# A decoder layer on one core: the input projection ends with a gate, attention's first keys, queries and scores are issued ahead of the samples' constants, and partial sums are added as they come

## The chip, the cores and the metric

The kernel runs on one core of a Trainium2 chip. The metric is device time in microseconds (us), the median of several runs of the same program. A core has TensorE (PE: matrix products into PSUM banks), VectorE (DVE), ScalarE (ACT), GpSimd (POOL) and SyncE (SP). Each engine works through its own list of instructions in order; semaphores between the lists make one wait for another. SP, ACT and POOL also issue DMAs, which move data between the core's memory and the chip's main memory.

## The reference

One layer of a decoder computes 1024 prompt tokens and 64 sample tokens (8 requests of 8 tokens, each with 4096 tokens in a paged cache). Cut to what matters here:

```python
h = rms_norm(x, norm1) * (1 + scale1) + shift1
z = h @ w_in
(q, kc, vc, ks, vs, kw, vw, gates, conv_bg, conv_cg, conv_h, pool_in) = jnp.split(z, IN_SPLITS, axis=-1)
q = rms_norm(q.reshape(B, T, N_KV_HEADS, Q_PER_KV, HEAD_DIM), q_gain)
...
k_cmp = rms_norm(compress(full[:, :, 0], cmp_pe[0], cmp_w1[0], cmp_w2[0]), k_gain[0])
v_cmp = compress(full[:, :, 1], cmp_pe[1], cmp_w1[1], cmp_w2[1])
o_cmp, p_cmp = cmp_attention(q, k_cmp, v_cmp, q_pos)
top_i, sel_ok = select_blocks(p_cmp, q_pos, -(-full.shape[1] // SLC_BLOCK))
o_slc = slc_attention(q, top_i, sel_ok, q_pos, full[:, :, 2], full[:, :, 3])
...
o_attn = (g[..., 0:1] * o_cmp + g[..., 1:2] * o_slc + g[..., 2:3] * o_win).reshape(B, T, ATTN_W)
u_ext = jnp.concatenate([conv_past, conv_cg * conv_h], axis=1)
y_conv = conv_bg * short_conv(u_ext, conv_w, conv_bias)
...
x = x + gate1 * (jnp.concatenate([o_attn, y_conv, y_pool], axis=-1) @ w_out)
h = rms_norm(x, norm2) * (1 + scale2) + shift2
x = x + gate2 * swiglu(h, w_up, w_down)
```

Attention has three branches: over keys that are compressed from blocks of 32 tokens, over blocks selected by the compressed scores, and over a sliding window of 512 tokens.

## The kernel before, in words

The layer runs in stages: norms and the input projection (with part of the compression of the samples' caches), attention of the prompt and of the samples side by side (with the rest of the compression), and the output projection with the feed-forward part. Products in fp32 are made as three products of split operands (`mm3`): an operand is split into a high part, written by ACT (`kh`, `qh`, `w_hi`, `mh`, L175), and a low part, written by DVE (`kl`, `ql`, `w_lo`, `ml`, L171).

The order of the work comes from a small planner in the kernel (`run`, `spawn`, `hold`, `use`, L59 on): each piece of work is a generator with a priority; the planner keeps an estimated clock for every engine and always continues the ready piece of lowest priority number. The framework's scheduler then fixes the list of each engine. What it decides is read from the lists, not from the order of the text.

**Input projection** (L884 to L956). The columns of `w_in` are handled in 16 tiles of 128, in the order of the list at L899; every tile is computed for three chunks of tokens (384, 384, 320). The consumer depends on the tile: `q0` to `q3`, `ks` and `kw` go through `head_norm`, which squares on ACT (L758), has PE average over a head (`h_sq,mean_h`), takes a root on ACT (L763), a RECIPROCAL on DVE (L766) and multiplies on DVE (L767). `cg`, `ch` and `bg` are the short convolution's three inputs: `cg` is copied by ACT, `ch` is multiplied and convolved on DVE, and `bg` is one DVE multiplication per chunk and a store. Two of these triples exist (0 and 1), and before the change they follow each other. While `q0` to `q3` run, a piece of work (`up_weights_ahead`, L959) forms split weights for the feed-forward part in the tiles `p_raw` and `p_hl` and stores them to main memory; `hold(formed == 2)` waits for it in the planner.

**Compression.** For each of the samples' 8 caches pages are loaded into `stream` buffers (L531, alternately by SP and POOL) and multiplied in "octets", which the trace shows as 32 rows of `bank<-stream`. The last compression of the prompt (`compress_prompt`, L592) has its matmuls in the projection stage.

**Attention** (`attention`, L1397). `masks` makes the masks of the prompt on POOL and DVE; `key_stacks` (L987) splits both key stacks, 1024 new and 64 compressed keys each; `query_parts` splits the first 128 queries; `constants3` and `sample_setup` (L1165) make the samples' constants; then the prompt's units start. A unit of `scores` (L1018) is one of 128 queries, half of the heads and a branch: PE multiplies keys and queries into two banks; DVE evicts with the mask added and a running minimum (L1068); ACT takes exp with a sum (L1080); DVE makes the gate over the sum (L1086); POOL scales `P` by it (L1090); PE transposes `P` (`ident,P`), and multiplies with the values.

**Samples** (L1296 to L1395). The samples are worked in four groups of two requests (`p`), with nine units each: eight of selected blocks and one of the window. A unit multiplies a loaded buffer (`unit`, or `stream` where one is free) with the queries `qb`, evicts, takes exp, transposes `e`, and multiplies with the values into one column of `part`. `sample_combine` starts after a group's last unit: it forms weights `cw`, then `co` as a sum of 12 columns (one TENSOR_SCALAR and 11 SCALAR_TENSOR_TENSORs, L1382), transposes it on PE, copies it to `smo` (L1389), and stores that to `mix_d` on SP's queue (L1393).

**Output projection** (L1446 on). Weights `w_raw` are loaded through three buffers on SP (L1443) and split; `mixc`, the mixers' outputs for 272 tokens, is fetched from `mix_d` (L1468: on SP for the first chunk, on ACT for the others) and split into `mh`, `ml`; ACT also issues the loads of the residual input, `x1a` and `x1b` (L1494).

## Time and profile before

| what | value |
|---|---|
| median of 3 runs | 1683.15 us (1681.12 to 1685.02) |
| profiled execution | 1672.63 us |
| its span, first to last instruction | 1671.0 us |
| mean granted TensorE clock | 0.977 of full speed |
| busy: PE, DVE, ACT, POOL | 93%, 65%, 47%, 40% of the span |
| DMA | 302.12 MB, mean 181 GB/s |

The durations below come from the one profiled execution; it ran 10.5 us below the median of the runs. Its span is what the time coordinates of the rows refer to. A row of a timeline has the start, the duration, the engine, the line of the kernel, the operation, the tiles (out<-in) and the shape; a bracket gives the engine's idle time ahead of the row and what ended it. "x32" stands for 32 alike instructions in succession. L12 is line 12 of the kernel before.

### The profile page before, as it was taken

The numbers are of one execution on the slowest core, as the hardware profiler recorded it, in microseconds if no ns is written. First come the engines' busy times: TensorE is split into PE (matmuls) and PEld (weight loads), VectorE is DVE, ScalarE is ACT, GpSimd is POOL, SyncE is SP. The second block draws the span as 40 slices with busy tenths as digits, with TensorE's granted clock in tenths as the row PEclk, the third lists the DMA queues.
The fourth block names the chain that finished last, engine by engine and source line by source line (L and its number), as shares of the span: only waits on it lengthen the run. The fifth ranks groups of instructions, "written<-read, shape, count | busy, mean of one in ns | idle before, by whom it ended". The sixth has DMA issues, their size and how long they took to land. (4 is left out here: it accounts for less than half of the span.)

```text
span 1671.0 us, 35661 instructions
## 1 busy us (share of the span) xinstructions
PE 1562.1 (93%) x12697; PEld 1391.8 (83%) x12697; DVE 1090.4 (65%) x2625; ACT 779.0 (47%) x1829; POOL 665.4 (40%) x789
## 2 busy tenths in 40 slices
PE   6899999997999899899599989999999999899998
PEld 2898997896777566566499989999999999899988
DVE  4723234777555666767579878777777775577695
ACT  3522115335765666666466534433434443344462
POOL 3120110114333123223013356554555455788695
PEclk9999999998999999999899999999999999999999
DMA  9585654425467363245685564446444335966553
GB/s 336 182 287 162 207 168 148 144 95 162 133 186 217 100 193 104 70 131 147 210 303 187 198 221 168 143 145 232 145 145 143 142 136 204 393 234 241 182 168 121
DMA packets 186834, 302.12 MB, mean 181 GB/s; under 512 B 26353, under 2 KB 114994, under 8 KB 186338
## 3 DMA queue, kind: packets, MB, share of 16 engines
q1 hardware_dynamic: 166786, 272.20, 49.1%
q0 software_dynamic: 5856, 16.24, 3.0%
q10 hardware_dynamic: 14016, 11.41, 2.2%
q8 instruction: 101, 1.65, 0.4%
q14 instruction: 75, 0.61, 0.1%
HBM read 233.43 MB, written 70.53 MB: 182 GB/s over the span
## 5 line engine op out<-in xcount | busy, mean ns | idle before, releaser
L139 PE MATMUL bank<-b_hi,w_hi 128*128 128x272 f32 x1232 | 351.8, 291 | 7.3 <-DVE f_g L1631 2.9
L139 PE MATMUL bank<-b_lo,w_hi 128*128 128x272 f32 x1232 | 353.8, 289 | 1.7 <-DVE b_lo L171 1.7
L139 PE MATMUL bank<-b_hi,w_lo 128*128 128x272 f32 x1232 | 348.9, 288 | 0.7 <-DVE w_lo L171 0.7
L139 PEld LDWEIGHTS bank<-b_hi,w_hi 128*128 128x128 f32 x1232 | 231.0, 189 | 10.6 <-ACT b_hi L175 4.7
L139 PEld LDWEIGHTS bank<-b_lo,w_hi 128*128 128x128 f32 x1232 | 232.8, 189 | 2.4 <-DVE b_lo L171 2.3
L139 PEld LDWEIGHTS bank<-b_hi,w_lo 128*128 128x128 f32 x1232 | 231.0, 189 | 0.9 <-DVE w_lo L171 0.9
L1090 POOL TENSOR_SCALAR P<-P,st 128x128 f32<-128x128 f32 (+10 forms) x192 | 109.5, 584 | 230.2 <-DVE st L1086 139.1
L171 POOL TENSOR_TENSOR w_s<-w_raw 128x512 f32<-128x512 f32 (+1 forms) x88 | 126.7, 1440 | 64.6 <-DVE w_lo L171 50.5
L171 DVE TENSOR_TENSOR w_lo<-w_raw,w_hi 128x512 fp32r<-128x512 f32 (+2 forms) x121 | 116.9, 975 | 53.8 <-ACT w_hi L175 50.7
L139 PEld LDWEIGHTS bank<-stream 128*128 128x128 f32 x1056 | 127.4, 198 | 17.9 <-issue 13.0
L175 ACT ACTIVATE w_hi<-w_raw 128x512 fp32r<-128x512 f32 (+2 forms) x122 | 80.9, 678 | 130.1 <-PE bank L139 78.2
L171 POOL TENSOR_TENSOR x<-x,d_m 128x272 f32<-128x272 f32 x144 | 126.6, 901 | 34.9 <-DVE x L1833 20.5
L139 PE MATMUL bank<-stream 128*128 128x128 f32 x1056 | 133.8, 284 | 6.2 <-DMA stream<-in_cacheA 5.7
L1080 ACT ACTIVATE P<-P,st 128x640 f32<-128x640 f32 (+12 forms) x192 | 112.7, 588 | 46.1 <-DVE st L1074 26.6
L139 PE MATMUL bank<-h_hi,w_hi 128*128 128x384 f32 (+1 forms) x384 | 130.1, 339 | 0.9 <-ACT py L879 0.6
L139 PE MATMUL bank<-g,w_hi 128*128 128x272 f32 x616 | 121.5, 293 | 8.3 <-DVE x L1833 6.5
L139 PE MATMUL bank<-h_hi,w_lo 128*128 128x384 f32 (+1 forms) x384 | 126.5, 330 | 0.0
L171 DVE TENSOR_TENSOR w_lo<-w_s,w_hi 128x512 fp32r<-128x512 f32 (+1 forms) x124 | 116.8, 944 | 14.8 <-ACT w_hi L175 12.6
L139 PE MATMUL bank<-h_lo,w_hi 128*128 128x384 f32 (+1 forms) x384 | 125.8, 328 | 0.0
L139 PE MATMUL bank<-g,d_hi 128*128 128x272 f32 x616 | 120.2, 291 | 2.6 <-DVE x L1833 1.7
L1833 DVE SCALAR_TENSOR_TENSOR x<-bank,mod,x 128x272 f32<-128x272 f32 (+1 forms) x192 | 87.3, 476 | 40.8 <-PE bank L139 35.5
L139 PEld LDWEIGHTS bank<-g,w_hi 128*128 128x128 f32 x616 | 98.2, 191 | 10.1 <-DVE x L1833 7.4
(371 smaller groups left out, 3732.3 us busy)
## 6 DMA issues: line engine op xcount, KB each, us to landing
g_d<-f_s SPq DMA_DIRECT2D x57, 544.0 KB, 3.3
g<-g_d SPq DMA_DIRECT2D x56, 544.0 KB, 6.3
wada<-in_wada SPq DMA_DIRECT2D x96, 256.0 KB, 5.4
stream<-in_cacheA SPq DMA_DIRECT2D x192, 128.0 KB, 3.2
w_raw<-in_wup SPq DMA_DIRECT2D x40, 512.0 KB, 4.5
unit<-in_cacheB SPq DMA_DIRECT2D x152, 128.0 KB, 2.4
stream<-in_cacheB SPq DMA_DIRECT2D x104, 128.0 KB, 2.4
w_raw<-in_wout SPq DMA_DIRECT2D x24, 512.0 KB, 4.6
```

What stands on the lines that cost most here:

```text
L139: return self.nc.tensor.matmul(out, lhsT, rhs, start=start, stop=stop, skip_group_check=chain)
L171: (self.nc.vector if eng == "dve" else self.nc.gpsimd).tensor_tensor(out, a, b, op=op)
L175: self.nc.scalar.activation(hi, src, AF.Copy)
L1080: nc.scalar.activation(Ps, Ps, AF.Exp, scale=-1.0, bias=sy[:, g, 0:1], accum_out=sy[:, g, 1:2])
L1090: nc.gpsimd.tensor_scalar(Ps, Ps, sy[:, g, 3:4], 0.0, op0=OP.mult, op1=OP.add)
L1833: nc.vector.scalar_tensor_tensor(out[:, :n], acc[:, :n], self.mod[:, 5, m, 0:1], out[:, :n], op0=OP.mult, op1=OP.add)
```

## The change

Five things move. (1) `compress_prompt` loads pages of the samples' compression right after its matmuls. (2) The projection's order becomes `kc vc cg0 ch0 bg0 p0 ks p1 kw q0 q1 cg1 ch1 q2 q3 bg1`, so that the last tile is a gate `bg1` instead of `q3`; the second convolution triple has a pool of its own, `conv1`, opened after the weights formed ahead. (3) `attention` loads ACT's exp table with a dummy instruction, `key_stacks` splits the first 128 new and the 64 compressed keys of the first stack, then the first queries, then the first 128 keys of the second stack, then the rest; the samples' constants and setup are issued after the planner has issued the first unit of scores. (4) `sample_combine` is started at the exp of a group's window unit: it adds ten columns when nine partial results are there, and the last column when its product is. (5) `smo` is stored on POOL's queue.

```diff
--- before.py
+++ after.py
@@ -613,6 +613,7 @@
                 self.mm(uv[:, kv, 0:P], self.w1[:, kv * KT + k, :], rv[:, kv, k], k == 0, k == KT - 1)
+        self.compress_load(EARLY * 4 + 1)
         r = self.compress_evac(uv[:, :, 0:P], vt, pre, 0, 8)
@@ -896,7 +897,7 @@
         self.zout = (zq_, zp_)
-        order = ["kc", "vc", "cg0", "ch0", "bg0", "cg1", "ch1", "bg1", "p0", "ks", "p1", "kw", "q0", "q1", "q2", "q3"]
+        order = ["kc", "vc", "cg0", "ch0", "bg0", "p0", "ks", "p1", "kw", "q0", "q1", "cg1", "ch1", "q2", "q3", "bg1"]
         self.ada2 = self.pool("ada2", "left")
@@ -937,11 +938,13 @@
             self.spawn(lambda: 0.9 if self.octets <= PACE * (self.z_steps - z0) else 1.5, self.compress_more())
+            def conv(cv, j):
+                st = dict(zip(("cg", "ch", "bg"), self.conv_steps(cv, j)))
+                return lambda nm, ch, acc, c0, n: st[nm[:2]](ch, acc)
             with self.pool("conv") as cv:
-                for j in range(2):
-                    st = dict(zip(("cg", "ch", "bg"), self.conv_steps(cv, j)))
-                    yield from tiles([n + str(j) for n in ("cg", "ch", "bg")],
-                                     lambda nm, ch, acc, c0, n: st[nm[:2]](ch, acc))
+                yield from tiles(["cg0", "ch0", "bg0"], conv(cv, 0))
             with self.pool("pooling") as pl:
@@ -951,8 +954,13 @@
                 self.spawn(0.6, self.up_weights_ahead(pp, 1))
-                yield from tiles(["q0", "q1", "q2", "q3"], qk)
+                yield from tiles(["q0", "q1"], qk)
                 yield from self.hold(lambda: self.formed == 2)
+            with self.pool("conv1") as cv:
+                step = conv(cv, 1)
+                yield from tiles(["cg1", "ch1"], step)
+                yield from tiles(["q2", "q3"], qk)
+                yield from tiles(["bg1"], step)
             yield from self.hold(lambda: self.prompt_at and self.heads == 18 and 5 in self.ada_at)
@@ -984,15 +992,23 @@
-    def key_stacks(self):
-        nc = self.nc
+    def key_parts(self, j, a, n):
+        kh, kl = self.K[j]
+        src = self.kcp[:, a:a + n] if a < 64 else self.ksw[:, j, a - 64:a - 64 + n]
+        self.split(kh[:, a:a + n], kl[:, a:a + n], src, n)
+    def key_stacks(self, ap):
+        self.key_parts(0, 64, P)
+        self.key_parts(0, 0, 64)
+        self.query_parts(ap, 0)
+        self.key_parts(1, 64, P)
         for j in range(2):
-            kh, kl = self.K[j]
-            for a, n, src in ((64, SEQ, self.ksw[:, j, 0:SEQ]), (0, 64, self.kcp)):
-                self.split(kh[:, a:a + n], kl[:, a:a + n], src, n)
-                yield max(self.t["dve"], self.t["act"]) - 1.0
-        self.stacks_at = max(self.t["dve"], self.t["act"])
+            self.key_parts(j, 64 + P, SEQ - P)
+        self.key_parts(1, 0, 64)
+        self.stacks_at = self.t["pe"] + 3.0
+        self.use("dve", 0.0, self.t["act"])
@@ -1090,6 +1106,7 @@
             yield 0.0
+        self.scored = u + 1
         self.spawn(0, self.values(pool, u, j, half, br, Pt, seg, ready + 0.1))
@@ -1171,8 +1188,6 @@
                 self.q[s, :, SEQ:].rearrange("p r (b t) -> p b r t", t=NT))
-        self.kn = pool.tile([P, 2, 64], F32, name="kn")
-        nc.vector.tensor_copy(self.kn, self.ksw[:, :, SEQ:])
         self.use("dve", 1.5)
@@ -1272,6 +1287,7 @@
         self.give("S", self.use("dve", 0.35, self.t["pe"]))
+        st["parts"] = st.get("parts", 0) + 1
@@ -1332,6 +1348,8 @@
             t = self.use("act", 0.36, t + 0.1, table="exp")
+            if x == 8:
+                self.spawn(2, self.sample_combine(pool, st, p))
             self.spawn(2, self.sample_values(pool, u, st, kv, e, nx, t + 0.2, src))
@@ -1349,16 +1367,20 @@
                         t == 0, t == 3)
-        self.give("a", self.evac(st["part"][:, nx], o[:, 0:P], P))
+        st["last_at"] = self.evac(st["part"][:, nx], o[:, 0:P], P)
+        self.give("a", st["last_at"])
         self.unit_free.append(src)
         self.u_done += 1
-        if u % 9 == 8:
-            yield from self.hold(lambda: self.u_done >= u + 1)
-            yield from self.sample_combine(pool, st, u // 9)
+        if nx < 9:
+            st["parts"] = st.get("parts", 0) + 1
+        else:
+            st["last"] = True
         nc = self.nc
+        yield from self.hold(lambda: st["parts"] == 9)
         nm, den, part, gr = st["nm"], st["den"], st["part"], st["gr"]
@@ -1378,9 +1400,12 @@
         nc.vector.tensor_scalar(o, part[:, 11], gr[:, 0:1], None, op0=OP.mult)
-        for c in range(11):
+        for c in (0, 1, 2, 3, 4, 5, 6, 7, 8, 10):
             nc.vector.scalar_tensor_tensor(o, part[:, c], w[:, c:c + 1], o, op0=OP.mult, op1=OP.add)
-        yield self.use("dve", 4.0, self.t["pe"]) + 0.5
+        yield self.use("dve", 3.7, self.t["pe"])
+        yield from self.hold(lambda: "last" in st)
+        nc.vector.scalar_tensor_tensor(o, part[:, 9], w[:, 9:10], o, op0=OP.mult, op1=OP.add)
+        yield self.use("dve", 0.3, st["last_at"]) + 0.2
         tr = yield from self.bank_of("S")
@@ -1390,26 +1415,30 @@
         self.give("S", self.use("dve", 0.4, self.t["pe"]))
-        nc.sync.dma_start(self.mix_d[:, 0:4, SEQ + 16 * p:SEQ + 16 * p + 16],
-                            mo.rearrange("p r b t -> p r (b t)"))
+        nc.gpsimd.dma_start(self.mix_d[:, 0:4, SEQ + 16 * p:SEQ + 16 * p + 16], mo.rearrange("p r b t -> p r (b t)"))
         self.combined = p + 1
     def attention(self, ap, kp_, opened):
+        with self.tc.issue_after(self.last_sqrt.ins):
+            self.nc.scalar.activation(self.warm, self.eps, AF.Exp)
+        self.table = "exp"
         self.masks(ap)
-        self.use("dve", 1.0)
-        yield from self.key_stacks()
-        self.query_parts(ap, 0)
-        with self.tc.issue_after(self.last_scale.ins):
-            self.constants3(ap)
-            self.sample_setup(ap)
-        self.use("dve", 5.0)
+        self.key_stacks(ap)
+        self.kn = ap.tile([P, 2, 64], F32, name="kn")
+        self.nc.vector.tensor_copy(self.kn, self.ksw[:, :, SEQ:])
         kp_.__exit__(None, None, None)
         self.spawn(lambda: 1.8 + self.v_done / 32, self.prompt_attention(pp))
+        yield from self.hold(lambda: self.scored >= 1)
+        self.constants3(ap)
+        self.sample_setup(ap)
+        self.use("dve", 4.0)
+        self.set_up = True
         self.spawn(share, self.compress(cp, batches, 0))
+        yield from self.hold(lambda: self.set_up)
         sp = opened.enter_context(self.pool("samp", "left"))
@@ -2122,7 +2151,10 @@
         self.cmp_tags = ("S", "a")
+        self.scored = 0
+        self.set_up = False
         with self.pool("att", "left") as ap:
+            self.warm = ap.tile([P, 1], F32, name="warm")
             self.K = [[ap.tile([P, 64 + SEQ], F32R, name=f"k{x}{j}") for x in "hl"] for j in range(2)]
```

The lists of the engines, as built, at the places that matter. PE behind the last matmul of the input projection's last tile (`h_hi`, `h_lo` are the normed input, `kh_…`, `kl_…` the key stacks: `kh_3506` before and `kh_3538` after are the first stack, `kh_3508` and `kh_3540` the second). Before, starting with the octet behind the norm's matmuls; the next row is an entry of 32 `stream` matmuls, that is two octets:

```order
L139 MATMUL bank<-stream 128x128 x16
L139 MATMUL bank<-kh_3506,qh 128x192 x2
L139 MATMUL bank<-kl_3507,qh 128x192 x2
L139 MATMUL bank<-kh_3506,ql 128x192 x2
L139 MATMUL bank<-kh_3506,qh 128x192 x2
L139 MATMUL bank<-kl_3507,qh 128x192 x2
L139 MATMUL bank<-kh_3506,ql 128x192 x2
L139 MATMUL bank<-kh_3508,qh 128x128 x2
L139 MATMUL bank<-kl_3509,qh 128x128 x2
L139 MATMUL bank<-kh_3508,ql 128x128 x2
L139 MATMUL bank<-kh_3508,qh 128x128 x2
L139 MATMUL bank<-kl_3509,qh 128x128 x2
```

The same place after the change:

```order
L139 MATMUL bank<-h_hi_102,w_lo 128x320
L139 MATMUL bank<-stream 128x128 x32
L139 MATMUL bank<-kh_3538,qh 128x192 x2
L139 MATMUL bank<-kl_3539,qh 128x192 x2
L139 MATMUL bank<-kh_3538,ql 128x192 x2
L139 MATMUL bank<-kh_3538,qh 128x192 x2
L139 MATMUL bank<-kl_3539,qh 128x192 x2
L139 MATMUL bank<-kh_3538,ql 128x192 x2
L139 MATMUL bank<-kh_3540,qh 128x128 x2
L139 MATMUL bank<-kl_3541,qh 128x128 x2
L139 MATMUL bank<-kh_3540,ql 128x128 x2
L139 MATMUL bank<-stream 128x128 x16
```

The two octets that followed the second stack's scores now stand ahead of the first stack's, in the place of one octet; a further octet stands between the two halves of the second stack's scores.

DVE ahead of the first scores' eviction (`kl_…` low parts of the key stacks, `ql` of the queries, `t_…` to `m_new` the samples' constants, `ISA P,st` the eviction). Before, the end of the constants and the first eviction:

```order
L342 SCALAR_TENSOR_TENSOR hind<-hi,hg 128x8
L1171 COPY qb<-q 64x8x32 x2
L314 SCALAR_TENSOR_TENSOR ok<-a,tv,ge 128x256
L323 TENSOR_SCALAR m_win<-w,tv 128x8
L304 COPY rsum<-eq 32x32 x4
L316 TENSOR_SCALAR m_new<-ok 128x256
L1068 ISA P,st<-bank,m_slc 128x128
L1068 ISA st 128x1
```

After the change, the same stretch; two copies of the compression (`pre`) stand between:

```order
L304 COPY rsum<-eq 32x32 x4
L314 SCALAR_TENSOR_TENSOR ok<-a,tv,ge 128x256
L331 TENSOR_SCALAR sel<-si 128x512
L340 TENSOR_SCALAR hg<-hi 128x8
L316 TENSOR_SCALAR m_new<-ok 128x256
L342 SCALAR_TENSOR_TENSOR hind<-hi,hg 128x8
L587 COPY pre<-bank 64x128
L588 COPY pre<-bank 64x128
L1084 ISA P,st<-bank,m_slc 128x128
L1084 ISA st 128x1
```

The constants still stand ahead of the first eviction.

ACT at the end of attention (`part` the evicted products of the last sample units, `w_hi` the output projection's weights, `x1a` the residual input, `mh` the mixers' outputs). Before:

```order
L161 ACTIVATE part<-bank 128x128
L175 ACTIVATE w_hi<-w_raw 128x512 x2
L161 ACTIVATE part<-bank 128x128
L175 ACTIVATE w_hi<-w_raw 128x512 x7
L1494 DMA x1a_10556<-in_xT 128x2x272 x3
L175 ACTIVATE mh<-mixc 128x272 x2
L1494 DMA x1a_10556<-in_xT 128x2x272
L175 ACTIVATE mh<-mixc 128x272 x2
L1494 DMA x1a_10557<-in_xT 128x2x272
L1468 DMA mixc<-mix_d 128x2x272
L1494 DMA x1a_10557<-in_xT 128x2x272
L1468 DMA mixc<-mix_d 128x2x272
```

After:

```order
L161 ACTIVATE part<-bank 128x128
L161 ACTIVATE spt<-bank 128x512
L161 ACTIVATE part<-bank 128x128 x2
L175 ACTIVATE w_hi<-w_raw 128x512 x8
L1523 DMA x1a_10566<-in_xT 128x2x272 x4
L1523 DMA x1a_10567<-in_xT 128x2x272 x2
L175 ACTIVATE mh<-mixc 128x272 x2
L175 ACTIVATE w_hi<-w_raw 128x512
L1523 DMA x1a_10567<-in_xT 128x2x272 x2
L175 ACTIVATE mh<-mixc 128x272 x2
```

Six loads of `x1a` instead of three now stand ahead of the first `mh`, and eight splits of weights ahead of those.

SP at the same place. Before:

```order
L531 DMA unit<-in_cacheB 128x256
L1293 DMA unit<-in_swinKV 128x2x1024
L1443 DMA w_raw<-in_wout 128x1024 x7
L1393 DMA mix_d<-smo 128x4x16
L1468 DMA mixc<-mix_d 128x2x272 x4
L1443 DMA w_raw<-in_wout 128x1024
```

After:

```order
L531 DMA stream<-in_cacheB 128x256
L1309 DMA stream<-in_swinKV 128x2x1024
L1472 DMA w_raw<-in_wout 128x1024 x6
L1497 DMA mixc<-mix_d 128x2x272 x4
L1472 DMA w_raw<-in_wout 128x1024 x2
L1542 DMA x_d<-x1a_10566 128x272
```

The store of `smo` is gone from SP's list, one `w_raw` load stands behind the fetches of `mixc`, and the last sample loads go into a `stream` buffer.

## Rows read from the trace of the kernel before

**Rows 1.** The page's busy table: each engine's busy time, share, instructions.

```profile
PE 1562.1 (93%) x12697; PEld 1391.8 (83%) x12697; DVE 1090.4 (65%) x2625; ACT 779.0 (47%) x1829; POOL 665.4 (40%) x789
```

**Rows 2.** Windows, all engines; columns in the first line, clock behind POOL.

```profile
core 0: us, PE busy (x) PEld busy (x) DVE busy (x) ACT busy (x) POOL busy (x), PEclk, DMA share, GB/s
373.50:391.50 18.00, 8.60 (x63) 7.22 (x61) 16.34 (x58) 6.13 (x11) 8.73 (x24) 0.72 0.51 147
391.50:396.00 4.50, 4.50 (x25) 4.49 (x25) 2.56 (x18) 4.02 (x24) 2.67 (x9) 0.59 0.41 119
400.00:800.00 400.00, 371.17 (x3753) 260.07 (x3752) 256.89 (x1105) 260.74 (x707) 126.18 (x217) 0.97 0.48 144
816.40:831.60 15.20, 0.47 (x1) 0.18 (x1) 7.78 (x18) 5.01 (x12) 0.00 (x0) 0.68 0.78 256
```

**Rows 3.** Timeline of PE at the transition: start, duration, instruction, [idle before <- releaser].

```profile
373.60 0.31 PE L139 MATMUL bank<-h_hi,w_lo 128*128 128x320 f32 x1
...
375.08 3.73 PE L139 MATMUL bank<-stream 128*128 128x128 f32 x32
...
379.79 0.35 PE L139 MATMUL bank<-kh,ql 64*128 64x192 f32 x2 [0.58 <-DVE ql L171]
385.30 0.53 PE L139 MATMUL bank<-kh,qh 64*128 64x192 f32 x2 [5.16 <-DVE q L767]
...
390.07 0.44 PE L139 MATMUL bank<-kh,qh 64*128 64x128 f32 x1 [3.66 <-DVE st L1068]
```

**Rows 4.** Timeline of DVE at the transition.

```profile
375.36 1.23 DVE L171 TENSOR_TENSOR kl<-kv__93,kh 128x1024 fp32r<-128x1024 f32 x1 [1.30 <-ACT kh L175]
...
380.26 4.55 DVE L766 RECIPROCAL h_sq<-h_sq 128x384 f32<-128x384 f32 x2
384.74 0.97 DVE L767 SCALAR_TENSOR_TENSOR q<-bank,qgain_s,h_sq 128x384 f32<-128x384 f32 x2
...
389.54 0.28 DVE L1068 CUSTOM_DVE_ANT_0 P<-bank,m_slc 128x128 f32<-128x128 f32 x1
```

**Rows 5.** Timeline of PE at the end of attention.

```profile
814.43 1.97 PE L139 MATMUL bank<-unit,spt 128*64 128x128 f32 x32 [0.65 <-DVE cs L1376]
823.27 0.47 PE L143 MATMUL bank<-ident,co 128*128 128x128 f32 x1 [6.88 <-DVE co L1382]
831.64 1.50 PE L139 MATMUL bank<-mh,w_hi 128*128 128x272 f32 x5 [7.89 <-ACT mh L175]
```

**Rows 6.** Timeline of ACT, one row of the transition and two of the end.

```profile
389.90 1.28 ACT L1080 ACT_TABLE_LOAD   x1 [11.41 <-issue]
...
824.41 1.55 ACTq L1494 DMA_DIRECT2D x1a<-in_xT  x3
831.16 0.43 ACT L175 ACTIVATE mh<-mixc 128x272 fp32r<-128x272 f32 x1 [6.19 <-DMA mixc<-mix_d]
```

**Rows 7.** Timeline of SP's queue at the end of attention.

```profile
808.16 16.01 SPq L1443 DMA_DIRECT2D w_raw<-in_wout  x7
826.09 0.38 SPq L1393 DMA_DIRECT2D mix_d<-smo  x1
826.52 2.05 SPq L1468 DMA_DIRECT2D mixc<-mix_d  x4
```

**Rows 8.** Lines of tile p_hl: duration min/median/max in ns, first and last start.

```profile
L980 SPq DMA_DIRECT2D w_d<-p_hl x1: 320/320/320, 352.3 to 352.3; - x1
```

**Rows 9.** Timeline of PE, the first matmul of the q tiles.

```profile
319.94 0.42 PE L139 MATMUL bank<-h_hi,w_hi 128*128 128x384 f32 x1 [0.35 <-DVE mod L394]
```

**Rows 10.** DMA issues, 805 to 835 us: KB each, median us to landing.

```profile
w_raw<-in_wout SPq DMA_DIRECT2D x7, 512.0 KB, 4.2
x1a<-in_xT ACTq DMA_DIRECT2D x8, 272.0 KB, 4.7
```

**Rows 11.** Timeline of POOL at the transition.

```profile
382.69 1.17 POOL L531 DMA_DIRECT2D stream<-in_cacheA  x2 [1.05 <-issue]
```

**Rows 12.** Waits of PE from 400 to 800 us: total, times, longest.

```profile
PE bank L143 <- POOL P L1090: 11.4, 5, 3.1
```

## The prediction

> **What bounds the kernel now.** I read the page's busy table first. TensorE (PE) is busy 93% of the span [rows 1], so time can come only from the stretches in which PE waits or runs at the lower of its two clock levels. The windows say where such stretches lie near the change [rows 2]: between the last projection matmul and the first steady attention work (373.5 to 391.5 us) PE works 8.60 of 18.00 us, and between attention's last matmul and the output projection's first (816.4 to 831.6) 0.47 of 15.20. In the 400 us between, PE lacks 400 − 371.17 = 28.8 us, in many small waits. The timelines of PE and of the engines that it waits for then give each wait its cause.
>
> Transition [rows 3]: the last projection matmul ends at 373.60 + 0.31 = 373.91 (call it E). PE then does the norm's matmuls, one compression octet (32 trace rows of `stream`, 3.73 us) and the first score matmuls, with idle pieces of 0.58, 5.16 and 3.66 us: 9.40 us in all. The waits are DVE's [rows 4]: it turns the last q tile's norm (two RECIPROCALs, 380.26 to 384.81, then q itself to 385.7), then builds constants, and evicts the first score only at 389.54, which is E + 15.6. The clock shows 0.72 over the stretch and 0.59 over the 4.50 us behind it [rows 2]. The clock's levels are 2.4 and 1.2 GHz: the 4.50 us lose 4.50 × (1 − 0.59) = 1.85, and of the busy time from 385.30 to 391.5 (6.2 us less the 3.66 of idle, 2.5, with overlaps up to 3) half is lost, 1.4. So **9.40 idle + 3.3 of clock = 12.7 us** is what the transition can return.
>
> End [rows 5]: the last weighted sum ends at 814.43 + 1.97 = 816.40 (call it X); PE waits 6.88 us for `co`, transposes it, and waits 7.89 us for `mh`; it starts the output projection at 831.64 = X + 15.24. `mh` itself waits for the `mixc` fetch [rows 6], which SP issues at 826.52 behind the store of `smo` [rows 7].
>
> **The change, part by part.**
>
> *Projection order.* The same matmuls run; gate bg1 instead of q3 comes last. What DVE does after E shrinks by RECIPROCAL and q of the last chunks, 380.26 to 385.7, 5.4 us [rows 4], and grows by two gate multiplications (128 × 384, nearest row: the 0.97 us of two q multiplications), 1.0. This is the largest piece of the transition. The second conv pool reuses the memory of `p_hl`, so that its first eviction waits for `p_hl`'s last store. That is issued at 352.3 [rows 8], 32.4 us after the first q matmul at 319.94 [rows 9]; with a landing of 4.2 to 4.7 us, as the loads have [rows 10], it is through near 37. The four q tiles took 54.0 us up to E, 13.5 each, so cg1's first chunk is done at 2.33 × 13.5 = 31.5 and waits some 5 us, while PE has two more chunks of cg1 (9 us) to cover it. I take 0; bounds −2 and +3.
>
> *First keys, queries and scores.* DVE's first key split waits no more for the 1024-wide `kh` (1.30 us [rows 4]) but for a 128-wide one: about 0.7 off. The splits come in more pieces, and two copies of the compression stand ahead of the first score: 0.8 on. But the order shows that the constants still stand on DVE **ahead** of the first score's eviction, though the text of the program issues them after it. So the first eviction goes from E + 15.6 to 15.6 − 5.4 + 1.0 − 0.7 + 0.8 = E + 11.3. PE has more to do till then: two octets of 3.73 us, twelve score matmuls in 1.3 (378.81 to 380.14) and the first half of K1's, 0.8: 9.6 us, behind a first wait of about 0.55 for DVE's gate. That leaves 11.3 − 9.6 − 0.55 = 1.1 till the eviction. The next octet needs two pages that POOL issues behind its masks; before, these went out at 382.69, E + 8.8, taking 1.17 [rows 11], and landings take 4.2 to 4.7 [rows 10], so E + 13 or so, another 1.2. For the first transposes of P, which one octet fewer covers, I add 0.9. Sum of idle: 0.55 + 1.1 + 1.2 + 0.9 = 3.7. Nothing in it is as long as the 5.16 us in which the clock fell; if the clock stays up, all 3.3 come back. Gain: 9.4 − 3.7 + 3.3 = 9.0; if the clock falls all the same, 5.7. I take **8**, nearer the upper end, since each piece of idle is shorter than the 3.66 us that followed that fall; bounds 5 and 11.
>
> *The exp table* (1.28 us) is loaded in ACT's idle time ahead of the splits: 0. The cover is the 11.41 us for which ACT stood idle before that load [rows 6].
>
> *Partial sums as they come.* Ten of the 11 products for `co` run ahead of the last weighted sum, so `co` should be ready 2 us behind X rather than 6.88. That would matter if `mh` waited for it. It waits for `mixc` columns of the prompt, and for SP and ACT. SP: the store moves to POOL. From SP's rows [rows 7] the store's own issue is 0.38 and SP stood from 824.17 (808.16 + 16.01) to 826.09 for its data: 1.9 + 0.4 = 2.3 us that `mixc` no longer waits.
> The Trainium skill ("DMA: Bandwidth & Descriptors", section "Issuing engines are not separate DMA queues") says that DMAs started by the sync, scalar and gpsimd engines run on the same 16 DMA engines, and that starting them from several engines saves only the sequencer's time to start them, which is usually small. By that rule the move would be worth the 0.4 us of the issue alone, and rival A below 1.9 us less (1671 rather than 1669); the rows say that the sequencer stood still as well, so I keep 2.3.
>
> The 2.3 us don't land in full, for the order shows two new waits. First, the last sample units now lie in `stream` buffers which the `w_raw` loads reuse: before, `w_raw` went out from 808.16, 8 us ahead of X; now the first waits for the last but one weighted sum (X − 1.0, half of the 1.97) and all others for the last. With landings of 4.2 us, splits of two halves, and three buffers, the third tile's split ends near X + 7.6, the sixth load goes out then, and `mixc` at X + 8.05 (before X + 10.1), landing near X + 13 (before X + 14.8). Second, ACT now issues six `x1a` loads ahead of the first `mh` (before, three); the fifth shares a semaphore lane with the first and waits for its landing. ACT gets to them when the fourth tile's weights are split, about X + 10.4; at 0.52 each (1.55 for three [rows 6]) and 4.7 us to landing [rows 10] the fifth goes at X + 15.6, and `mh` follows with 0.43: PE restarts near **X + 16.2**, a loss of 1.0. Bounds: −2 (ACT not held, `mixc` at X + 13) and +4 (landings of 7).
>
> *The middle.* All sample work between is dealt anew by the planner, with the same matmuls. I take 0 of its 28.8 us of idle; from waits of at most 3.1 us there [rows 12], bounds −6 and +6.
>
> **Sum:** −8 + 1 + 0 + 0 = −7 us on the profiled 1672.63, so 1665.6. That execution lies 10.5 us below the median of the three runs, 1683.15; the same difference gives **1676**. About 0.2% (3.4 us) is what a measurement of this kernel can tell from no change.
>
> **The rivals.**
>
> A. *The end opens too.* If the `w_raw` loads land as early as before and ACT is not held by `x1a`, only the `mixc` fetch behind X counts. For it speaks that the longest wait of the kernel (7.89) hangs on nothing but queue order; against it, the order of ACT and the buffers' reuse. PE would restart near X + 9, 6 to 7 us earlier; with the transition −14: 1669. Chance 0.17.
>
> B. *The stall only moves.* DVE's constants still precede the first eviction, and the scores wait behind them; PE then idles in one long piece before the third octet, if its pages land at E + 17 instead of 13, and the clock falls again. The transition returns 3 to 4 us, the end takes 1 to 2, net −2: 1681. For it: POOL has all masks to make before it issues the pages, as before. Chance 0.20.
>
> C. *Slower: the new deal in the middle starves the transposes of P.* They wait for POOL's scaling of P, 11.4 us in five waits, 2.3 each [rows 12]. The sample side starts later now and its units fall elsewhere between the prompt's; where a unit's transposes come with no sample work ahead, such a wait is open. It decides from (7 + 3.4) / 2.3, some 4.5 more waits on, which is twice as many as before; with five, +11.5 − 7 = +4.5: 1687.6. Against it: PE's queue has the same filler in sum. Chance 0.13.
>
> **How the numbers follow.** The forecast has 0.50, its own range 1671 to 1681 (−12 to −2); 0.05 of it lies within 0.2%. Faster: 0.45 + 0.17 = 0.62, and 0.01 from B's better end, 0.63; same: 0.05 + 0.19 = 0.24; slower: 0.13. The range reaches into A (down to 1667, two thirds of it) and C (up to 1686).
>
> **What would show it.** In the profile after: between the last projection matmul and the second group of P's transposes, idle pieces that sum to about 4 us and a granted clock near 1; two octets in a row straight behind the gate; the first score evicted near E + 11. At the end `co` within 2 us of the last weighted sum, and yet a first output-projection matmul near X + 16, waiting for ACT's `mh`, whose own wait is the ACT queue. I am wrong if that restart comes before X + 12, if the transition shows a half-clock stretch, or if PE's idle between 400 and 800 differs by over 6 us.

## The result, and the profile after

The changed kernel takes 1690.3 us (median of 20 runs, 1683.18 to 1696.07), the kernel before 1680.87 (20 runs): the ratio is 1.006, interval 1.0047 to 1.0073. The change costs some 10 us where 7 were to be gained. The profiled execution of the changed kernel took 1688.57 us (span 1687.0).

The first profile of the kernel before, on which the prediction rests, was a quick execution: 1672.63 us against its median of 1680.87. Both kernels were therefore profiled a second time (e13, e17). E is the end of the last projection matmul, T the first transposes of P, X the last weighted sum of the samples, R the first matmul of the output projection.

| stretch | before | before, 2nd | after | after, 2nd | difference of the means |
|---|---|---|---|---|---|
| start to 75 us | 75.0 | 75.0 | 75.0 | 75.0 | 0 |
| 75 us to E | 298.9 | 299.5 | 311.7 | 312.9 | +13.1 |
| E to T | 26.7 | 26.8 | 23.4 | 22.5 | −3.8 |
| T to X | 415.8 | 424.1 | 421.6 | 426.8 | +4.3 |
| X to R | 15.2 | 15.9 | 17.7 | 17.2 | +1.9 |
| R to the end | 839.4 | 843.3 | 837.7 | 838.6 | −3.2 |

The stretches sum to +12.3 us, the medians say +9.4. The largest loss lies ahead of E, in the projection; the transition gives back less than a third of it (it now also holds a further octet, 3.7 us, which stood behind T before). The two executions of one kernel differ by up to 8.3 us in the stretch T to X, most of it at half clock, so small differences there prove nothing.

The transition after, as PE's timeline shows it ([rows 3] are the same place before):

```profile
387.24 7.41 PE L139 MATMUL bank<-stream 128*128 128x128 f32 x64 [0.58 <-DVE cy L811]
394.58 0.36 PE L139 MATMUL bank<-kh,qh 64*128 64x192 f32 x2
...
396.74 0.29 PE L139 MATMUL bank<-kh,qh 64*128 64x128 f32 x1 [1.17 <-DVE st L1084]
...
399.63 6.20 PE L139 MATMUL bank<-stream 128*128 128x128 f32 x32 [2.37 <-DMA stream<-in_cacheA]
```

DVE's first score eviction behind the gate's last multiplication ([rows 4]), and POOL's page loads ([rows 11]):

```profile
386.69 0.49 DVE L811 TENSOR_TENSOR cy<-cy,bank 128x320 f32<-128x320 f32 x1 [2.96 <-PE bank L139]
...
396.21 0.29 DVE L1084 CUSTOM_DVE_ANT_0 P<-bank,m_slc 128x128 f32<-128x128 f32 x1
```

```profile
395.11 1.16 POOL L531 DMA_DIRECT2D stream<-in_cacheA  x2 [1.05 <-DMA stream<-in_cacheA]
396.96 1.12 POOL L531 DMA_DIRECT2D stream<-in_cacheA  x2 [0.70 <-issue]
```

E is 386.66 here. Three idle pieces, 0.58 + 1.17 + 2.37 = 4.12 us, stand where 9.40 stood; the third octet waits for its pages and starts at E + 12.97. It then takes 6.20 us instead of 3.7: the clock fell after all (granted clock 0.59 from 399.6 to 405.8 us).

The projection, in windows of both kernels (the first number is the window's length, the second PE's busy time; the first of the last three is the granted clock). Before:

```profile
78.00:92.00 14.00, 14.00 (x104) 14.00 (x104) 3.79 (x10) 4.16 (x7) 5.46 (x6) 1.00 0.93 312
125.00:135.00 10.00, 6.05 (x40) 5.55 (x40) 1.52 (x6) 2.77 (x5) 0.23 (x1) 0.83 0.79 243
208.00:226.00 18.00, 18.00 (x133) 16.56 (x133) 9.11 (x19) 3.48 (x5) 3.64 (x6) 1.00 0.42 111
270.00:326.00 56.00, 52.50 (x315) 42.28 (x314) 34.74 (x52) 23.26 (x44) 6.35 (x11) 1.00 0.50 160
```

After:

```profile
78.00:92.00 14.00, 14.00 (x95) 14.00 (x94) 3.50 (x10) 4.16 (x7) 5.26 (x6) 0.88 0.92 304
125.00:135.00 10.00, 5.14 (x26) 4.98 (x25) 1.91 (x6) 3.09 (x6) 1.08 (x2) 0.66 0.90 264
208.00:226.00 18.00, 15.56 (x85) 10.17 (x78) 8.09 (x11) 4.90 (x7) 0.55 (x1) 0.81 0.43 127
270.00:326.00 56.00, 49.96 (x329) 41.37 (x320) 34.45 (x46) 32.63 (x54) 9.18 (x10) 1.00 0.61 209
```

With busy × (1 − clock) as the loss at half clock, the four windows lose 1.7, 4.86 + 1.75, 2.44 + 2.96 and 6.04 us against 0, 3.95 + 1.03, 0 and 3.50: 11.3 us more. With q3's norm matmuls, 1.5 us that now lie ahead of E, that is 12.8, near E's shift of 386.66 − 373.91 = 12.75; that it comes so close is luck, for the windows were picked. (The first window's 1.7 is chance: the second profile of before has it too.) What stands behind the largest difference, in 208 to 226, is a chain over three engines, DVE, ACT and PE:

```profile
209.58 2.86 DVE L870 SCALAR_TENSOR_TENSOR pe_x<-pe_s,pe_x 64x1208 f32<-64x1208 f32 x2 [3.72 <-DMA out_poolS<-pe_x]
212.47 0.28 DVE L587 COPY pre<-bank 64x128 f32<-64x128 f32 x1
...
213.49 0.69 DVE L622 TENSOR_TENSOR pre<-pre,vt 128x510 f32<-128x510 f32 x1
```

```profile
214.26 1.28 ACT L624 ACT_TABLE_LOAD   x1 [6.49 <-DVE pre L622]
215.55 0.72 ACT L624 ACTIVATE vt<-pre,pec 128x512 f32<-128x512 f32 x1
```

```profile
216.32 0.73 PE L139 MATMUL bank<-vt,c_w 64*64 64x256 f32 x6 [2.17 <-ACT vt L624]
```

The pooling overwrites its input `pe_x` in place, and must wait until `pe_x` is stored. In the new order the pooling falls on a compression: its `pre` stands behind the waiting DVE, `vt` behind `pre`, PE behind `vt`, and PE runs on at half clock for part of the window (granted clock 0.81).

The end after: PE ([rows 5]), ACT ([rows 6]), SP ([rows 7]). X is 831.61.

```profile
829.64 1.97 PE L139 MATMUL bank<-stream,spt 128*64 128x128 f32 x32
834.32 0.33 PE L143 MATMUL bank<-ident,co 128*128 128x128 f32 x1 [2.71 <-DVE co L1407]
849.34 1.05 PE L139 MATMUL bank<-mh,w_hi 128*128 128x272 f32 x3 [14.69 <-ACT mh L175]
```

```profile
840.43 0.94 ACTq L1523 DMA_DIRECT2D x1a<-in_xT  x2
...
841.39 7.14 ACTq L1523 DMA_DIRECT2D x1a<-in_xT  x4
848.86 0.43 ACT L175 ACTIVATE mh<-mixc 128x272 fp32r<-128x272 f32 x1 [7.29 <-DMA x1a<-in_xT]
```

```profile
830.78 9.51 SPq L1472 DMA_DIRECT2D w_raw<-in_wout  x6
840.34 5.80 SPq L1497 DMA_DIRECT2D mixc<-mix_d  x4
```

`co` is ready 2.7 us behind X instead of 6.9, and nobody is there to use it: `w_raw` starts at X − 0.8 instead of X − 8.2, and the output projection at X + 17.7 instead of X + 15.2. The landings are slower as well: by the DMA view of 828 to 850 us, the median of `x1a` is 6.7 us (before 4.7) and that of the first `mixc` fetches 8.0 (before, from 805 to 835 us, 5.1).

### The profile page after: what moved, and what is told of

It reads as the page before. It is cut to its first block, busy times and chain, and to the rows that moved or that the text cites. A ratio compares the mean times of both kernels' runs of the same rounds, so it can differ in the third digit from the quotient of the medians.

```text
span 1687.0 us, 35640 instructions
## 1 busy us (share of the span) xinstructions
PE 1570.5 (93%) x12697; PEld 1393.9 (83%) x12697; DVE 1090.1 (65%) x2621; ACT 782.9 (46%) x1837; POOL 664.5 (39%) x793
## 4 chain that ended last, share of the span: by engine, by line
PE 41%; DVE 7%; DMA 4%; ACT 2%; issue 2%; POOL 1%; ACTq 0%; DVEq 0%; POOLq 0%
PE bank L139 40%; DVE w_lo L171 2%; PE bank L143 1%; DVE x L1862 1%; DMA w_raw<-in_wup 1%; DMA x1a<-in_xT 1%; DMA x1b<-in_xT 1%; DVE P L1084 1%; DMA x<-x_d 1%; DVE d_lo L171 1%; ACT w_hi L175 1%; POOL w_s L171 0%; DVE b_lo L171 0%; ACT P L1096 0%; DMA w_raw<-in_wout 0%
## 5 line engine op out<-in xcount | busy, mean ns | idle before, releaser
L139 PEld LDWEIGHTS bank<-stream 128*128 128x128 f32 x1056 | 130.0, 202 | 22.5 <-issue 13.8
L139 PE MATMUL bank<-stream 128*128 128x128 f32 x1056 | 136.9, 288 | 11.4 <-DMA stream<-in_cacheA 8.2
L1096 ACT ACTIVATE P<-P,st 128x128 f32<-128x128 f32 (+10 forms) x192 | 112.8, 589 | 45.9 <-DVE st L1084 23.4
```

Of the source, the lines that this page charges most:

```text
L139: return self.nc.tensor.matmul(out, lhsT, rhs, start=start, stop=stop, skip_group_check=chain)
L1096: nc.scalar.activation(Ps, Ps, AF.Exp, scale=-1.0, bias=sy[:, g, 0:1], accum_out=sy[:, g, 1:2])
```

## The experiments

Ratios are to the kernel before, with the 95% interval.

**The parts alone.** Four kernels carry one part each of the change's diff: e1 the order (the hunks of `input_projection`), e2 the combination (`sample_values`, `sample_combine`), e3 all but these two (the changed kernel with the old ones), e4 one line:

```diff
+        self.compress_load(EARLY * 4 + 1)
```

> The kernel before with the projection's new order and the second convolution pool alone. Theory P (the loss is made in the projection stage: in the profile after, the last projection matmul ends 12.8 us later, of it 4.7 us more idle time and 5.8 us more loss at half clock): 6 to 11 us slower than before, with the last projection matmul near 384 to 387 us of the span; the norm's RECIPROCALs being gone from the transition gives back up to 5 us, so that the whole may read only 2 to 6 slower. Theory S (the loss is made on the samples' side, by the combination and the new deal of units; the projection's difference is chance): within 3 us of before in the projection, and up to 5 us faster in all, for the transition is shorter.

> The kernel before with the partial sums added as they come and the store of smo on POOL alone. Theory P: small, -1 to +4 us; the output projection starts 16 to 18 us behind the last weighted sum instead of 15.2, although co is ready within 3 us of it. Theory S: 5 to 12 us slower than before, most of it between 400 and 830 us of the span.

> The changed kernel with the old projection order and the old combination: what is left of the change is attention's beginning (first keys, queries, scores, the exp table, the constants behind them) and the early page load. Theory P: the transition still ends with q3's norm, so DVE has the 5.4 us of RECIPROCALs ahead again, but the scores come early: 0 to 5 us faster than before. Theory S: 3 us slower to 3 us faster, since the sample side starts later.

> The kernel before with the early load of compression pages alone. Theory P and theory S both: within 3 us of before; PE's wait for stream pages between the first scores and the next octet may go, and pages that arrive early may push others back by as much.

| run | ratio | E | E to T | T to X | X to R | R to end |
|---|---|---|---|---|---|---|
| e1 order | 1.0044 [1.0027, 1.0061] | 386.9 | 20.4 | 428.5 | 17.1 | 839.1 |
| e2 combination | 0.9941 [0.9923, 0.9958] | 373.3 | 26.7 | 412.4 | 11.8 | 848.5 |
| e3 attention and load | 1.0060 [1.0041, 1.0079] | 375.4 | 27.2 | 426.8 | 12.6 | 844.7 |
| e4 load | 1.0137 [1.0116, 1.0159] | 374.1 | 23.5 | 434.8 | 12.1 | 852.6 |

The order shifts E as theory P says, and it alone also gives the shorter transition. The combination, for which theory S expected a cost and theory P next to nothing, is the one good part: 10 us faster. In that run the samples end ahead of the prompt's last unit, so the first `w_raw` and `mixc` go out at 800 us, 24 us ahead of the first output matmul. Part of that is paid back behind R: the stretch R to the end is 848.5 us instead of 839 to 843, and PE waits there for splits of weights (4.46 us in one piece at 848.59). Neither theory foresaw what attention's part costs. The load alone is the worst of the four, and why is open (below). The three parts (e1, e2, e3), +0.44, −0.59 and +0.60%, sum to +0.45; measured was +0.60 [0.47, 0.73].

**The projection.** e5 moves the pooling early and keeps q3 last; e6 has the gate last and the pooling late; e7 is the changed kernel with the pooling's result in the sum's tile; e14 is e1 with the same edit.

```diff
+        order = ["kc", "vc", "cg0", "ch0", "bg0", "p0", "ks", "p1", "kw", "cg1", "ch1", "bg1", "q0", "q1", "q2", "q3"]
...
+        order = ["kc", "vc", "cg0", "ch0", "bg0", "q0", "q1", "q2", "q3", "p0", "ks", "p1", "kw", "cg1", "ch1", "bg1"]
```

```diff
-                nc.vector.scalar_tensor_tensor(e[r_, 15:], sg[r_, 15:], iw, e[r_, 15:], op0=OP.mult, op1=OP.subtract)
+                nc.vector.scalar_tensor_tensor(s[r_, 15:], sg[r_, 15:], iw, e[r_, 15:], op0=OP.mult, op1=OP.subtract)
...
-                self.mm(m[:, :np_], pw, e[:, 15 + c0:15 + c0 + np_], True, True)
+                self.mm(m[:, :np_], pw, s[:, 15 + c0:15 + c0 + np_], True, True)
```

> The kernel before with the second convolution triple moved behind the pooling and the projection still ending with q3 (kc vc cg0 ch0 bg0 p0 ks p1 kw cg1 ch1 bg1 q0 q1 q2 q3). It has the early pooling without the gate at the end. Theory P1 (the projection loses because the pooling now falls on the compression: DVE waits 3.4 us for the store of pe_x, the compression's pre stands behind it, PE waits for vt and then runs at half clock): the last projection matmul ends 6 to 13 us later than before and the transition keeps its 26.7 us, so 6 to 12 us slower than before. Theory P2 (the projection loses because cg1, ch1 and the q tiles are mixed and the weights formed ahead have two q tiles as cover): within 3 us of before.

> The kernel before with the order kc vc cg0 ch0 bg0 q0 q1 q2 q3 p0 ks p1 kw cg1 ch1 bg1: the gate is last, the pooling is as late as before or later. Theory P1: the last projection matmul ends within 4 us of before, the transition is 5 to 6 us shorter, so 0 to 6 us faster than before. Theory P2: also faster, by the same. Theory N (any order but the old one costs, since the old one was fitted to the planner's numbers): 4 us slower or more, with stalls at other places of the projection.

> The changed kernel, with the pooling's difference written to its sum's tile instead of over pe_x, so that DVE does not wait for the store of pe_x. Theory P1: the wait of 3.4 us on DVE near 208 us goes, PE's wait for vt near 216 us (2.2 us) and the half clock behind it (3 us) go, and the last projection matmul ends 4 to 6 us earlier; 3 to 6 us faster than the changed kernel, that is 4 to 7 us slower than before. Theory P2: within 2 us of the changed kernel, 8 to 12 us slower than before.

> The kernel before with the new projection order and the pooling's difference in a tile of its own. Theory P1 (the store of pe_x that DVE waits for is what the early pooling costs): the last projection matmul near 380 to 382 us instead of 387, 4 to 6 us faster than the order alone (+0.44%), so 1 to 4 us slower than before. Theory P2: as the order alone, 5 to 10 us slower than before.

The window 208 to 226 of e1, e5, e7 and e14, one line each in that order:

```profile
208.00:226.00 18.00, 15.88 (x84) 11.08 (x83) 8.08 (x11) 4.91 (x7) 0.55 (x1) 0.81 0.46 148
```

```profile
208.00:226.00 18.00, 16.05 (x86) 10.45 (x85) 5.96 (x10) 6.75 (x10) 0.55 (x1) 0.81 0.31 106
```

```profile
208.00:226.00 18.00, 17.83 (x119) 13.81 (x117) 6.57 (x13) 7.20 (x11) 0.58 (x2) 1.00 0.61 186
```

```profile
208.00:226.00 18.00, 17.83 (x120) 13.36 (x122) 5.62 (x9) 7.46 (x11) 1.62 (x3) 1.00 0.62 196
```

Early pooling brings the stall, also with q3 last; without the in-place write nearly all of it is gone, idle and half clock. E moves from 386.7 to 381.8 (e7) and from 386.9 to 380.6 (e14); the times go from 1.0060 to 1.0032 [1.0015, 1.0048] and from 1.0044 to 1.0013 [0.9998, 1.0029]. With the new order this edit is thus worth about 5 us, half of what the change costs. (E is 381.8 on average over e7, e12, e14 and e16, which have the edit, and lies between 384.9 and 387.9 in the kernels with the same order without it.) P1 is right on that and wrong on its size: e5 (1.0078 [1.0061, 1.0095]) has the stall, yet its E is 373.0, so the early pooling alone does not make E late, and what e5 loses it loses behind T (T to X 431.2 us); and e6 (1.0050 [1.0031, 1.0069]) with the pooling late has E at 381.1 with other stalls (PE waits 4.62 us for the pooling itself and 2.02 us for `vt`), as theory N forecast; the reason that N gives, an order fitted to the planner's numbers, was not shown. Of the rest of E's shift, 1.5 us is the moved norm and some 4 us lie in the window 270 to 326 (e7: idle 5.92 and half clock 1.50, against 3.50 before). No run undid those, and their cause is open.

**The end.** e8 issues `x1a` and `x1b` on POOL's queue; e10 keeps the last two sample units in `unit` buffers; e9 lets the prompt end later; e12 is e9 with the mended pooling.

```diff
-                nc.scalar.dma_start(dst, src)
+                nc.gpsimd.dma_start(dst, src)
```

```diff
-            src = self.unit_free.pop(0)
+            if self.unit_next >= 34 and "unit" not in self.unit_free:
+                break
+            src = "unit" if self.unit_next >= 34 else self.unit_free[0]
+            self.unit_free.remove(src)
```

```diff
-        self.spawn(lambda: 1.8 + self.v_done / 32, self.prompt_attention(pp))
+        self.spawn(lambda: 1.8 + 1.2 * self.v_done / 32, self.prompt_attention(pp))
```

> The changed kernel with the loads of x1a and x1b issued on POOL's queue instead of ACT's. Theory E1 (at the end, mh is late because ACT's queue stands in front of it with six x1a loads of which the later ones wait for the earlier ones' landing): the output projection starts 12 to 14 us behind the last weighted sum instead of 17.7, 3 to 5 us faster than the changed kernel. Theory E2 (mh is late because the mixc fetch is late, behind w_raw loads that wait for the last sample units' buffers): still 16 to 18 us behind it, within 2 us of the changed kernel.

> The changed kernel with the last two sample units kept in the unit buffers, so that the stream buffers, whose memory w_raw reuses, come free earlier; the samples still end last. Theory W: the first w_raw loads go out several us ahead of the last weighted sum, the output projection starts 11 to 15 us behind it instead of 17.7, 2 to 6 us faster than the changed kernel. Theory M: within 2 us of the changed kernel, since loading with two buffers makes the last units wait for their pages.

> The changed kernel with one number of the planner changed: the prompt's priority rises with 1.2 instead of 1.0 over its progress, so that the samples' last unit, not the prompt's, is the earlier one to end. Theory W (the end is late because the samples end last: the buffers that the w_raw loads reuse are then free only with the last weighted sum, and w_raw and mixc cannot be loaded ahead, as they were in the run with the combination alone): the output projection starts within 8 us of attention's last matmul instead of 17.7, and the whole is 5 to 10 us faster than the changed kernel, near before. Theory M (the loss lies in the middle, in the samples' delayed start, and the end only takes it over): the end gets shorter, but the middle longer by as much; within 3 us of the changed kernel.

> The changed kernel with the pooling's difference in a tile of its own and the prompt's priority rising with 1.2. Theory P1 with W: the gains add, 5 us from the projection and 5 to 10 us from the end, so that the whole is 0 to 6 us faster than before. Theory M: 4 to 6 us slower than before, as with the pooling mended alone.

e8: 1.0109 [1.0090, 1.0129], R at X + 20.5: neither theory. All loads of `x1a` now leave at once, and the DMA view from 828 to 855 us shows what they do to `mixc`:

```profile
w_raw<-in_wout SPq DMA_DIRECT2D x7, 512.0 KB, 5.8
x1a<-in_xT POOLq DMA_DIRECT2D x8, 272.0 KB, 6.4
x1b<-in_xT POOLq DMA_DIRECT2D x5, 272.0 KB, 8.7
mixc<-mix_d SPq DMA_DIRECT2D x4, 272.0 KB, 15.0
```

The Trainium skill ("DMA: Bandwidth & Descriptors", "Issuing engines are not separate DMA queues") says that DMAs of all issuing engines run on the same 16 DMA engines; this trace agrees, with 15.0 us for `mixc` against 8.0 in the changed kernel.

e10 confirms what makes the end late. Its PE and SP:

```profile
848.58 1.09 PE L139 MATMUL bank<-unit,spt 128*64 128x128 f32 x16 [1.05 <-ACT spt L161]
854.70 0.48 PE L143 MATMUL bank<-ident,co 128*128 128x128 f32 x1 [5.02 <-DVE co L1410]
855.80 1.50 PE L139 MATMUL bank<-mh,w_hi 128*128 128x272 f32 x5 [0.62 <-ACT mh L175]
```

```profile
819.35 0.34 SPq L1475 DMA_DIRECT2D w_raw<-in_wout  x1
836.84 12.18 SPq L1475 DMA_DIRECT2D w_raw<-in_wout  x5
849.08 2.13 SPq L1500 DMA_DIRECT2D mixc<-mix_d  x4
```

With `w_raw` out 13 us ahead of X, R is at X + 6.1. But T to X takes 439.3 us, and the whole 1.0090 [1.0067, 1.0113]. So W's mechanism is shown for the start of the output projection, and M's remark holds here that a shorter end bought by a new deal of the units is paid in the middle. e9 (1.0151 [1.0132, 1.0171]) and e12 (1.0126 [1.0101, 1.0150]) meet neither forecast. The prompt ends last in them, with 7 us of its work between X and R, but `w_raw` still goes out only with the last weighted sum (e9: 828.65, X is 828.61). PE starts the output projection 10.5 and 8.9 us behind the prompt's last matmul, where W said 8 at most, and then waits again: R to the end is 853.3 and 851.9 us instead of 838, while T to X is 421.0 and 424.9, no longer than in the changed kernel.

**Attention's part.** e11 takes the new beginning without the load and without holding the samples back.

```diff
-        yield from self.hold(lambda: self.scored >= 1)
-        self.constants3(ap)
+        with self.tc.issue_after(self.last_scale.ins):
+            self.constants3(ap)
```

> The kernel before with attention's new beginning alone, without the early page load, and with the samples' constants and setup ahead of the prompt's units, so that the samples' side is not held until the first unit of scores. Theory H (what costs in the attention part is that the samples start later, and the early page load that goes with it): the transition is 0 to 3 us shorter than before, the stretch from the first transposes to the last weighted sum stays within 5 us of before's 415.8, and the whole within 4 us of before, 6 us or more faster than attention's beginning with the load. Theory K (the keys in pieces themselves cost): 6 us or more slower than before, as the run with the load.

Measured: 1.0135 [1.0113, 1.0156], T to X 444.6. Theory H falls: it isn't the late start alone. K's forecast, 6 us or more slower, came in, but its reason is not shown: the new beginning alone (+1.35%) and the load alone (+1.37%) are each worse than both together (e3, +0.60%), so neither has a price of its own. The 135 us from T on, for before, e2 (combination), the changed kernel, e3 and e4, each its own line:

```profile
400.58:535.58 135.00, 129.63 (x1192) 99.80 (x1192) 78.68 (x364) 91.01 (x269) 46.66 (x99) 0.97 0.59 176
```

```profile
400.07:535.07 135.00, 129.92 (x1181) 100.07 (x1181) 78.67 (x364) 91.35 (x271) 46.85 (x99) 0.96 0.58 176
```

```profile
410.01:545.01 135.00, 122.17 (x1072) 90.74 (x1073) 69.08 (x312) 85.25 (x244) 43.48 (x91) 0.96 0.58 177
```

```profile
402.62:537.62 135.00, 122.04 (x1072) 90.83 (x1073) 69.04 (x312) 85.20 (x244) 43.36 (x91) 0.96 0.58 177
```

```profile
397.56:532.56 135.00, 125.07 (x1091) 96.43 (x1092) 68.51 (x314) 82.56 (x246) 45.94 (x100) 0.94 0.58 178
```

PE is idle 5.4 and 5.1 us before and in e2, 12.8 and 13.0 with attention's part and the load, 9.9 with the load alone: in the changed kernel what the transition gains is idle again within 135 us, in waits of at most 2.4 us for ACT (`pt`, `vt`) and for pages. But such idle time is no mark of the load or of the keys. The same stretch in e11 (keys, no load) and in e5 (nothing but another order in the projection):

```profile
394.98:529.98 135.00, 120.09 (x1086) 94.88 (x1086) 66.39 (x311) 84.85 (x248) 43.99 (x93) 0.95 0.57 173
```

```profile
400.39:535.39 135.00, 121.70 (x1114) 94.38 (x1113) 70.87 (x317) 81.66 (x244) 43.20 (x92) 0.95 0.57 173
```

That is 14.9 and 13.3 us; e1 has 8.7, e18 7.5, and e14 and e16 5.3 and 5.6. Many edits ahead of T cost something behind it, and which part of an edit costs what was not isolated.

**What parts make together.** e13 and e17 are the two kernels again (table above). e15 is e2 with the mended pooling, e16 order, combination and mended pooling, e18 order and combination, each composed of the edits shown.

> The kernel before, unchanged, profiled a second time. If the first profile was a lucky execution (1672.6 us against a median near 1680): a span 4 to 12 us longer, the projection's last matmul within 2 us of 373.9, and the stretch from the first transposes to the last weighted sum at 420 to 426 us with more loss at half clock and the same waits. If the order of the middle is what makes the difference: 414 to 418 us again.

> The changed kernel, unchanged, profiled a second time. If the account by stretches holds: the last projection matmul again near 385 to 388 us, the first transposes 23 to 24 us later, the output projection 17 to 18.5 us behind the last weighted sum. The stretch between may move by up to 8 us with the loss at half clock, as it did between the two profiles of the kernel before.

> The kernel before with the combination alone and the pooling's difference in a tile of its own, the old order. Theory P1: with the old order the pooling's wait falls on nothing that PE waits for, except the 1.5 us near 286 us; so 8 to 12 us faster than before, as the combination alone.

> The new order, the combination and the pooling's difference in a tile of its own, without attention's new beginning and without the early load. Theory A (the parts add, and the attention part with its load is what turns the sum): 5 to 10 us faster than before. Theory B (the parts don't add; any two of them together lose what the combination gains): within 3 us of before or slower.

> The new projection order and the combination without attention's new beginning and without the early load. If the parts add (order +0.44%, combination -0.59%): 0 to 5 us faster than before, with the samples ending ahead of the prompt as in the run with the combination alone, and the attention part with its load then accounts for the 10 to 14 us up to the changed kernel. If they don't add: 3 us or more slower than before.

e13: 1.0004 [0.9985, 1.0022], the stretch T to X at 424.1 us: the first profile was a lucky one. e17: 1.0094 [1.0059, 1.0128], the account by stretches holds. e18: 1.0009 [0.9992, 1.0027], e16: 0.9972 [0.9956, 0.9988]; from e18 to the changed kernel it is 0.5%, which is attention's part with its load, near the 0.6% of e3. e15, expected 8 to 12 us faster, is 1.0017 [1.0004, 1.0030]: the mending, worth 5 us with the new order, undoes the combination's gain with the old one. The loss is not in the projection (E is 373.29, in e2 373.32) but at the transition, where e15's engines have another order. PE's rows of e15:

```profile
385.14 6.53 PE L139 MATMUL bank<-stream 128*128 128x128 f32 x32 [10.52 <-DVE t L289]
...
411.79 1.62 PE L139 MATMUL bank<-stream 128*128 128x128 f32 x6 [5.34 <-DMA stream<-in_cacheA]
```

In e2 the first of these octets starts at 374.49 without a wait, and PE doesn't wait for pages at the second place. POOL issues the pages behind the transition at 391.97 in e15 and at 382.10 in e2. So the mending moves more than the one wait that it was made for, and its 5 us with the new order hold for that order alone. The combination alone (e2) stays the fastest kernel, ahead of both.

## Why the prediction was wrong

- **The step that failed** is *Projection order*: "I take 0; bounds −2 and +3". It was +13.1, of it 1.5 the moved norm. I followed the wait that I had looked for, `p_hl`'s store in front of cg1's first eviction: it came (1.36 us on ACT) and PE did not feel it, as priced. But the change also moved the pooling ahead by three tiles, onto a compression, and I took "the same matmuls" for the same time. e7 and e14 give about 5 us of the 11.6 to the in-place write of the pooling, behind which DVE waits for a DMA; the rest, of it some 3 to 4 us in the window 270 to 326, stays without a cause.
- **The transition** was right: gate last takes 5.4 us of RECIPROCAL and q away, constants still precede the first eviction (E + 9.6, predicted 11.3), pages set the third octet (E + 12.97, predicted 13), idle 4.12 us (predicted 3.7). That sum is partly luck: the wait for pages was 2.37 us instead of 1.2, and the 0.9 for the transposes of P did not come. And the clock did not stay up. By idle and half clock (busy × (1 − clock), summed over windows of 2 us), 12.5 us of loss (12.7 in e13) became 6.7 (5.5 in e17): 6.5 gained, 8 predicted, in the bounds. But the order alone gives most of it: the same count leaves 7.0 us in e1 and 8.2 in e18. The early keys and scores add 1 to 2 us.
- **The end**: mechanism right (`w_raw` late by the buffers, ACT held by the fifth `x1a`, `co` early for nobody), size 1.0 against 1.9, within the bounds, with landings of 6.7 us (`x1a`) and 8.0 (`mixc`) where the sum took 4.7 and some 5. I missed that the deciding question is who ends last.
- **The middle**, taken as 0 with ±6, was off as well: +4.3 between means although one octet, 3.7 us, has moved ahead of T, so some 8. Whole times point there too: attention's part with its load costs 0.5 to 0.6% (e3, and e18 to the changed kernel), about what the order costs and what the combination gains. In the changed kernel some 6 us more idle stand in the 135 us behind T; e5 and e11 show that other edits bring as much, and the cause is open.
- **The rivals**: A did not come (its "longest wait of the kernel", 7.89 us, leaves out PE's 9.82 us ahead of its first matmul); B did not (the transition did gain, though the clock fell); C would have shown more waits for POOL's P: they total 11.4 us from 400 to 800, in six waits instead of five. The right sign came by a path that no rival named.
- With −6.5 for the transition, +11.6 for the projection, +8 for the middle, +1.9 for the end and −3.2 behind R the sum is +11.8; the medians say +9.4.

## What to carry to other kernels

A step that is moved takes its waits along: price what each of its instructions waits for at the new place, and who stands behind it on that engine, not only its work. An in-place write behind a store puts a DMA's landing on the engine. Before rating a stretch of one profile, profile the kernel twice; a chain that becomes early is worth only what the next chain (here the loads of weights, by whose buffers come free last) allows.

## What was not expected of the hardware

PE's granted clock can differ between two executions of the same list. In 78 to 92 us it stood at 0.88 in three of the four profiles of the two kernels and at 1.00 in the fourth, with PE's records busy for 14.00 of 14.00 us each time. In all four, PE runs 32 matmuls with only two columns each just ahead (3.6 to 3.7 us), and then an octet's matmuls, 22 of which take 4.1 to 4.3 us where the clock falls and 2.70 where it doesn't (the first profile of before). The changed kernel:

```profile
79.29 3.63 PE L139 MATMUL bank<-c_peT,stream 128*128 128x2 f32 x32
82.78 4.13 PE L139 MATMUL bank<-stream 128*128 128x128 f32 x22
```

Why it fell in one execution and not in the other, these traces don't show. And two executions of the same kernel differ by 13.6 us of span (1671.0 and 1684.6), with 29.5 and 28.8 us of idle time in T to X: most of that difference is the granted clock there (9.5 and 21.4 us of loss), not the waits.
